# Gate, up and down projections as seven half-size products instead of eight

## The chip, the cores and the metric

The kernel runs on one core of one Trainium2 chip. Five engines matter: TensorE (PE in the profile, its weight loads apart as PEld), VectorE (DVE), ScalarE (ACT), GpSimd (POOL) and SyncE (SP), whose queue issues the DMA transfers here. The metric is the device time of one execution in microseconds, the median of several runs.

## What is computed

One decoder layer over 512 tokens with 2048 features, all in float32. The mixing sub-layer comes first; the change touches what follows it:

```python
x = x + g_m[:, None, :] * mix
h = modulate(rms_norm(x, norm_ffn_g[l]), sh_f, sc_f)
gate, up = jnp.split(h @ w_gu[l], 2, axis=-1)        # 2048 -> 2 x 5632
x = x + g_f[:, None, :] * ((jax.nn.silu(gate) * up) @ w_down[l])   # 5632 -> 2048
return rms_norm(x, final_norm_g)
```

`sh_f`, `sc_f` and `g_f` are columns of `silu(c) @ w_ada + b_ada` (the modulation columns).

## The kernel before

Features lie on the 128 partitions and the 512 tokens along the free dimension. A feature vector of 2048 is 16 tiles (`KT`), the hidden vector of 5632 is 44 (`FT`). Float32 products are made from float32r parts: `split_into` (L103 to L106) writes `hi` on ACT and the remainder `lo` on DVE, and `mm3` (L122 to L126) issues three matrix products, hi x hi, hi x lo and lo x hi, each of 128 x 128 weights by 512 columns. `load_split` (L112) loads up to 1024 columns of weights through SP's queue into one of the `raw` buffers and splits them, under `high_priority`, into `whi` and `wlo`; `gemm_steps` (L128) runs them over all k.

`channel` (L912) first ends the output projection (`project`), in which every second step also makes a quarter of one of the modulation columns 68 to 79; each finished tile of x1 is squared into `acc`. Then come the norm, `modulate` for 16 tiles of h, and four chunks of the hidden vector with 11 tiles each: for each tile 16 k of gate and 16 of up into two PSUM banks, `Silu`, the product with up and its split; then 16 output tiles of `down` over the chunk's 11 k, each added into x1 in SBUF with the gate column g_f (L969). In the first chunk the last 16 modulation columns are made beside gate and up. Last come the final norm, 16 multiplications (L975) and the stores (L977).

The program is traced in this order, and a list scheduler puts each engine's instructions in the order in which it expects them to be ready, earlier-traced and high-priority ones first. Each engine, and SP's queue, then runs its list strictly in that order and waits where data or a buffer isn't ready. A pool's tiles of one tag share its `bufs` buffers.

The memory pool `big` holds 32 tiles of 128 x 512, for h (hi and lo), later for the split y and for x1.

## Time and profile before

| | us |
|---|---|
| median of 3 runs | 2512.42 (2512.3 to 2514.79) |
| span of the profiled execution | 2515.8 |
| PE busy in it | 2413.9 |
| DVE busy | 1380.4 |
| ACT busy | 843.7 |
| POOL busy | 82.0 |

The span is that of one execution under the profiler, from the first to the last instruction; no other time of that execution is given. Busy time counts an engine's instructions with their overlaps once. PE's matrix products are pipelined: their starts are measured, their ends modelled, so the spacing of starts says how fast PE runs, not the recorded length of one.

### The profile page before, as it was taken

What the parts mean: (1) busy time and instruction counts of PE and PEld (TensorE: products, weight loads), DVE (VectorE), ACT (ScalarE), POOL (GpSimd) and SP (SyncE); (2) the same over time, 40 slices, a digit from 0 to 9 for tenths busy, and PEclk for the clock granted to TensorE, in tenths of its full rate; (3) what the DMA queues carried; (4) which work ended last, traced back from release to release, by engine and by line L of the source; (5) the groups of instructions that cost most, each with busy time, mean ns of one, the idle gap of its engine ahead of it and who ended that gap; (6) DMA issues with size and microseconds to landing.
All of it is one profiled execution on the core that took longest, in us unless ns stands there. A gap on an engine that the chain in (4) does not pass through costs nothing.

```text
span 2515.8 us, 30983 instructions
## 1 busy us (share of the span) xinstructions
PE 2413.9 (96%) x11560; PEld 1953.4 (78%) x11560; DVE 1380.4 (55%) x3111; ACT 843.7 (34%) x1340; POOL 82.0 (3%) x131
## 2 busy tenths in 40 slices
PE   5999999999999999899999999999999999999997
PEld 3677777877777886687788888888888888888885
DVE  7979898999969847854423322233322233222244
ACT  4357364455355333432222222222222222222221
POOL 0000111111101000000000000000000000000000
PEclk9999998999999999999999999999999999999998
DMA  8864444444342438366423332323333233333233
GB/s 304 308 219 130 148 128 143 131 152 144 125 135 81 143 108 283 119 195 194 160 90 95 108 100 93 101 83 98 106 98 99 89 92 105 101 93 100 85 95 112
DMA packets 138938, 333.22 MB, mean 132 GB/s; under 512 B 15458, under 2 KB 28898, under 8 KB 134690
## 3 DMA queue, kind: packets, MB, share of 16 engines
q1 hardware_dynamic: 138788, 331.25, 40.7%
q8 instruction: 90, 1.47, 0.2%
q14 instruction: 60, 0.49, 0.1%
HBM read 322.92 MB, written 7.87 MB: 131 GB/s over the span
## 4 chain that ended last, share of the span: by engine, by line
PE 72%; DVE 9%; DMA 7%; issue 1%; ACT 1%; SPq 0%; POOL 0%; DVEq 0%; ACTq 0%
PE ps_mm L124 10%; PE ps_mm L126 10%; PE ps_mm L125 10%; PE ps_gr L126 6%; PE ps_st L124 6%; PE ps_gr L124 6%; PE ps_st L126 6%; PE ps_gr L125 6%; PE ps_st L125 6%; DMA adaq<-in_w_ada 6%; DVE adaq L199 2%; DVE wlo L106 2%; DVE rw_xp L764 1%; DVE rw_x L766 1%; DMA wraw<-in_w_out 1%
## 5 line engine op out<-in xcount | busy, mean ns | idle before, releaser
L106 DVE TENSOR_TENSOR wlo<-wraw,whi 128x1024 fp32r<-128x1024 f32 (+2 forms) x552 | 496.7, 902 | 730.2 <-ACT whi L105 721.1
L105 ACT CAST whi<-wraw 128x1024 fp32r<-128x1024 f32 (+2 forms) x552 | 436.6, 792 | 1292.4 <-PE ps_mm L125 401.1
L124 PE MATMUL ps_mm<-hhi,whi 128*128 128x512 f32 x1020 | 417.1, 410 | 9.8 <-ACT hhi L251 7.2
L126 PE MATMUL ps_mm<-hhi,wlo 128*128 128x512 f32 x1020 | 407.2, 399 | 1.7 <-DVE wlo L106 1.6
L125 PE MATMUL ps_mm<-hlo,whi 128*128 128x512 f32 x1020 | 406.5, 399 | 0.8 <-DVE hlo L252 0.7
L124 PEld LDWEIGHTS ps_mm<-hhi,whi 128*128 128x128 f32 x1020 | 193.4, 190 | 53.2 <-ACT hhi L251 9.9
L125 PEld LDWEIGHTS ps_mm<-hlo,whi 128*128 128x128 f32 x1020 | 193.7, 190 | 43.4 <-DVE hlo L252 4.8
L126 PEld LDWEIGHTS ps_mm<-hhi,wlo 128*128 128x128 f32 x1020 | 193.8, 190 | 42.3 <-DVE wlo L106 3.0
L199 DVE SCALAR_TENSOR_TENSOR adaq<-adaq,cbq 128x512 f32<-128x512 f32 x256 | 173.5, 687 | 92.9 <-DMA adaq<-in_w_ada 85.1
L126 PE MATMUL ps_gr<-hhi,wlo 128*128 128x512 f32 x496 | 193.7, 390 | 3.1 <-DVE wlo L106 3.1
L126 PE MATMUL ps_st<-hhi,wlo 128*128 128x512 f32 x496 | 193.6, 390 | 2.0 <-DVE wlo L106 2.0
L124 PE MATMUL ps_st<-hhi,whi 128*128 128x512 f32 x496 | 194.0, 391 | 1.6 <-ACT hhi L251 1.6
L125 PE MATMUL ps_gr<-hlo,whi 128*128 128x512 f32 x496 | 193.5, 390 | 0.0
L125 PE MATMUL ps_st<-hlo,whi 128*128 128x512 f32 x496 | 193.5, 390 | 0.0
L124 PE MATMUL ps_gr<-hhi,whi 128*128 128x512 f32 x496 | 192.6, 391 | 0.0
L126 PEld LDWEIGHTS ps_gr<-hhi,wlo 128*128 128x128 f32 x496 | 93.4, 188 | 23.6 <-DVE wlo L106 4.1
L126 PEld LDWEIGHTS ps_st<-hhi,wlo 128*128 128x128 f32 x496 | 93.4, 188 | 21.8 <-DVE wlo L106 2.5
L124 PEld LDWEIGHTS ps_st<-hhi,whi 128*128 128x128 f32 x496 | 93.5, 188 | 21.6 <-ACT hhi L251 2.2
L125 PEld LDWEIGHTS ps_gr<-hlo,whi 128*128 128x128 f32 x496 | 93.7, 189 | 19.6
L124 PEld LDWEIGHTS ps_gr<-hhi,whi 128*128 128x128 f32 x496 | 93.7, 189 | 19.4
L125 PEld LDWEIGHTS ps_st<-hlo,whi 128*128 128x128 f32 x496 | 93.3, 188 | 19.8 <-DVE hlo L252 0.3
L766 DVE TENSOR_TENSOR rw_x<-rw_x,rw_xp 128x27 f32<-128x27 f32 (+23 forms) x496 | 94.7, 196 | 5.7
(312 smaller groups left out, 3809.6 us busy)
## 6 DMA issues: line engine op xcount, KB each, us to landing
wraw<-in_w_gu SPq DMA_DIRECT2D x176, 512.0 KB, 3.6
adaq<-in_w_ada SPq DMA_DIRECT2D x256, 256.0 KB, 3.3
wraw<-in_w_in SPq DMA_DIRECT2D x160, 256.0 KB, 3.0
ada<-in_w_ada SPq DMA_DIRECT2D x32, 1024.0 KB, 7.2
wraw<-in_w_down SPq DMA_DIRECT2D x64, 512.0 KB, 3.5
wraw<-in_w_out SPq DMA_DIRECT2D x64, 256.0 KB, 3.3
wraw<-in_w_down SPq DMA_DIRECT2D x64, 192.0 KB, 2.3
x<-in_x SPq DMA_DIRECT2D x32, 256.0 KB, 5.3
```

The costliest lines, as they stand in the source:

```text
L105: nc.scalar.copy(out=hi, in_=src)
L106: nc.vector.tensor_tensor(out=lo, in0=src, in1=hi.bitcast(F32), op=ALU.subtract)
L124: mm(ps, lhsT=w[0], rhs=x[0], start=start, stop=False)
L125: mm(ps, lhsT=w[0], rhs=x[1], start=False, stop=False)
L126: self.pe = mm(ps, lhsT=w[1], rhs=x[0], start=False, stop=stop).ins
L199: nc.vector.scalar_tensor_tensor(out=t, in0=t, scalar=1.0, in1=cb, op0=ALU.mult, op1=ALU.mult, accum_out=part[:, m, h:h + 1])
L764: tt(out=pr[:, :n, :j], in0=at[:, s + 1:, s:s + 1].to_broadcast([P, n, j]), in1=x[:, s:s + 1, :j].to_broadcast([P, n, j]), op=ALU.mult)
L766: tt(out=x[:, s + 1:, :j], in0=x[:, s + 1:, :j], in1=pr[:, :n, :j], op=ALU.add)
```

## The change

Gate, up and down are computed with a scheme of seven products (Strassen's, in Winograd's form) on 2 x 2 blocks: the tokens are cut into two halves of 256, the features (k) into two halves, and the columns into two, which are the gate and the up tile of one m, or the output tiles m and m + 8 of down. Eight block products become seven, of sums and differences of blocks.

- `group` makes one such pair of output tiles. It loads four blocks of weights (128 x 1024; in down 128 x 1024 or 128 x 896), forms four sums of them (two on POOL, two on DVE), splits seven blocks into hi and lo, multiplies each by 256 columns over n k (8 or 7), and combines the seven results on the way out of PSUM (one copy on ACT, seven additions and subtractions on DVE).
- `operands` splits the seven blocks on the activations' side, once for a stage: `from_h` for h, `from_s` for a chunk of the hidden vector. Their eight sums (tiles of 128 x 4 x 256) are made on POOL.
- h is modulated in halves of 256 tokens, in place in x1's tiles. x1 therefore goes to DRAM (`x1d`) and is loaded, updated and stored again by each down chunk; the hidden vector goes to DRAM too (`sd`) and is loaded by halves. There are three chunks of down (16, 14 and 14 tiles) where four were.
- The operands of a stage are made beside the last group of the stage before. The first two groups are interleaved product by product.
- The last 16 modulation columns are made beside groups 4 and after, two quarters in each.
- `big` holds 8 tiles of 128 x 4 x 512, which `quad_view` gives out by quarters. The weights' pool has 10 `raw` buffers of 1024 columns and three each of `whi` and `wlo`; it is opened before the end of the output projection.

```diff
+    def quad_view(self, k, name, dtype):
+        if k % 4 == 0:
+            self.quad[name] = self.big.tile([P, 4, S], dtype, tag="h", name=name)
+        return self.quad[name][:, k % 4]
...
-        self.big = ctx.enter_context(tc.tile_pool(name="big", bufs=32))
-        self.open_weights(ctx, "wm", 512, 3, 3)
-        self.wm = self.wp
+        self.big = ctx.enter_context(tc.tile_pool(name="big", bufs=8))
+        self.quad = {}
+        self.wmctx = ExitStack()
+        self.open_weights(self.wmctx, "wm", 512, 3, 3)
         self.psum = ctx.enter_context(tc.tile_pool(name="psum", bufs=1, space=PSUM))
...
+        self.wmctx.close()
+        self.open_weights(ctx, "wf", 1024, 10, 3)
+        self.fq = fq = ctx.enter_context(tc.tile_pool(name="fq", bufs=2))
+        self.acc = acc = fq.tile([P, S], F32, name="sqacc", bufs=1)
+        self.x1d = [self.dram.tile([P, S], F32, name=f"x1d{m}") for m in range(KT)]
...
+            def done(m):
+                self.square(acc, xt[m], m, fp)
+                nc.sync.dma_start(out=self.x1d[m], in_=xt[m])
+            self.after_project = done
+            mods = self.mod_steps(range(64 + 4, 80), fp, ("ft", 2, "ad", 4))
...
-        for cf in range(NC):
-            s = []
-            for f in range(FC):
-                m = cf * FC + f
-                pg, pu = ps(), ps()
-                self.gemm(pg, i["w_gu"][2 * m], h)
-                self.gemm(pu, i["w_gu"][2 * m + 1], h)
...
-            if cf == 0:
-                with self.tc.issue_after(last):
-                    self.mod_cols(range(80, 96), self.wm, ("raw", 3, "raw", 3))
-            for m in range(KT):
-                p = ps()
-                self.gemm(p, i["w_down"][cf, m], s)
-                stt(out=xt[m], in0=p, scalar=self.mod[:, 80 + m:81 + m], in1=xt[m],
-                    op0=ALU.mult, op1=ALU.add)
-                if cf == NC - 1:
-                    self.square(acc, xt[m], m, fp)
...
+        chunks = [(0, 8), (16, 7), (30, 7)]
...
+        def modulate(q, side):
+            sl = slice(side * 256, side * 256 + 256)
+            for z in range(4):
+                k = 4 * q + z
+                v = quads[q][:, z, sl]
+                stt(out=v, in0=v, scalar=self.cols[:, 16 + k:17 + k], in1=rstd[:, sl],
+                    op0=ALU.mult, op1=ALU.mult)
+                nc.scalar.activation(out=v, in_=v, func=AF.Identity, bias=self.mod[:, 48 + k:49 + k])
...
+        def from_h(p):
+            if p == 1:
+                modulate(0, 0)
+                modulate(1, 0)
+                return [view(0, 0), view(1, 0)]
+            if p == 2:
+                modulate(2, 0)
+                modulate(3, 0)
+                return [view(2, 0), view(3, 0)]
+            if p == 6:
+                for j in range(2):
+                    modulate(j, 1)
+                    modulate(2 + j, 1)
+                    t = self.staging()
+                    pool_tt(out=t, in0=view(j, 1), in1=view(2 + j, 1), op=ALU.subtract)
+                    pool_tt(out=view(j, 1), in0=view(j, 0), in1=view(j, 1), op=ALU.subtract)
+                    pool_tt(out=view(j, 0), in0=t, in1=view(j, 0), op=ALU.subtract)
+                    s1.append(t)
+                return [view(0, 0), view(1, 0)]
+            if p == 5:
+                return s1
+            if p == 7:
+                return [view(0, 1), view(1, 1)]
+            if p == 4:
+                return [view(2, 1), view(3, 1)]
+            s4 = [self.staging(), self.staging()]
+            for j in range(2):
+                pool_tt(out=s4[j], in0=view(2 + j, 0), in1=view(j, 0), op=ALU.add)
+            return s4
...
+                    if p in (1, 2, 4):
+                        r.append(load(p != 1, p == 4, j))
+                    elif p == 6:
+                        t, u = load(0, 1, j), load(1, 1, j)
+                        pool_tt(out=t, in0=t, in1=u, op=ALU.subtract)
+                        u = load(0, 0, j)
+                        pool_tt(out=u, in0=t, in1=u, op=ALU.subtract)
+                        kept.append(t)
+                        r.append(u)
+                        v = load(1, 0, j)
+                        pool_tt(out=v, in0=v, in1=u, op=ALU.add)
+                        nc.sync.dma_start(out=self.s4[j][:, :v.shape[1]], in_=v)
+                    elif p == 7:
+                        t, u = load(0, 0, j), load(0, 1, j)
+                        pool_tt(out=t, in0=t, in1=u, op=ALU.subtract)
+                        r.append(t)
+                    else:
+                        t = self.staging()[:, :min(4, n - 4 * j)]
+                        nc.sync.dma_start(out=t, in_=self.s4[j][:, :t.shape[1]])
+                        r.append(t)
...
+        def gu_end(m, g, u):
+            nc.scalar.activation(out=g, in_=g, func=AF.Silu)
+            nc.vector.tensor_tensor(out=g, in0=g, in1=u, op=ALU.mult)
+            nc.sync.dma_start(out=where[m], in_=g)
+        last = {}
+        def down_end(c):
+            def end(m, g, u):
+                for t, k in ((g, m), (u, m + 8)):
+                    x = fq.tile([P, S], F32, tag="x1", name="x1t", bufs=2)
+                    nc.sync.dma_start(out=x, in_=self.x1d[k])
+                    stt(out=x, in0=t, scalar=self.mod[:, 80 + k:81 + k], in1=x, op0=ALU.mult, op1=ALU.add)
+                    if c == len(chunks) - 1:
+                        self.square(acc, x, k, fq)
+                        last[k] = x
+                    if c < len(chunks) - 1 or m < 7:
+                        nc.sync.dma_start(out=self.x1d[k], in_=x)
+            return end
...
+        def gu_src(m):
+            a, b = i["w_gu"][2 * m], i["w_gu"][2 * m + 1]
+            return a[:, :1024], b[:, :1024], a[:, 1024:], b[:, 1024:]
...
+        mods = self.mod_steps(range(80, 96), fq, ("ft", 2, "x1", 2))
+        self.ngroup = 0
+        order = (1, 2, 6, 5, 7, 4, 3)
+        g0, g1 = self.group(stages[0], 0), self.group(stages[0], 1)
+        for p in order[:-1]:
+            self.operands(stages[0], p)
+            next(g0)
+            next(g1)
+        self.operands(stages[0], 3)
+        for g in (g0, g1):
+            for _ in g:
+                pass
+        for z, st in enumerate(stages):
+            nxt = stages[z + 1] if z + 1 < len(stages) else None
+            for m in range(2 if z == 0 else 0, st["count"]):
+                g = self.group(st, m)
+                final = m == st["count"] - 1
+                for p in order:
+                    if p == 3 and final and nxt is None:
+                        self.reload(last)
+                    next(g, 0)
+                    if final and nxt is not None:
+                        self.operands(nxt, p)
+                    if z == 0 and m >= 4 and p in (6, 4):
+                        next(mods, 0)
...
+        for k in (7, 15, *[k for k in range(KT) if k not in (7, 15)]):
+            stt(out=last[k], in0=last[k], scalar=self.vec("final_norm_g", k), in1=rstd,
+                op0=ALU.mult, op1=ALU.mult)
+            nc.sync.dma_start(out=self.out[:, k], in_=last[k])
...
+    def reload(self, last):
...
+            v = self.quad_view(k, "xend", F32)
+            if k not in (7, 15):
+                self.nc.sync.dma_start(out=v, in_=self.x1d[k])
+                last[k] = v
...
+    def staging(self):
+        t = self.wp.tile([P, self.wc], F32, tag="raw", name="stage", bufs=self.wb[0])
+        return t.rearrange("p (k n) -> p k n", n=256)
...
+    def operands(self, stage, p):
+        at = {1: 0, 2: 2, 6: 4, 5: 6, 7: 8, 4: 10, 3: 12}[p]
+        out = []
+        for j, src in enumerate(stage["get"](p)):
+            if 4 <= at + j < 10:
+                t = self.cp.tile([P, 4, S], F32R, tag="c", name="comb")
+            else:
+                t = self.big.tile([P, 4, S], F32R, tag="h", name="comb")
+            n = src.shape[1]
+            t = t.rearrange("p k n -> p (k n)").rearrange("p (h k n) -> p h k n", h=2, n=256)
+            self.split_into(t[:, 0, :n], t[:, 1, :n], src)
+            out.append(t)
+        stage["ops"][p] = out
...
+    def group(self, stage, m):
+        nc, tc = self.nc, self.tc
+        tt, pool_tt = nc.vector.tensor_tensor, nc.gpsimd.tensor_tensor
+        n = stage["n"]
+        N = n * P
+        par = self.ngroup % 2
+        self.ngroup += 1
+        raw = []
+        for src in stage["src"](m):
+            t = self.wp.tile([P, self.wc], F32, tag="raw", name="wraw", bufs=self.wb[0])[:, :N]
+            raw.append(t)
+        for z in (0, 2, 1, 3):
+            nc.sync.dma_start(out=raw[z], in_=stage["src"](m)[z])
+        b11, b12, b21, b22 = raw
+        def product(tag, p, w):
+            with tc.high_priority():
+                hi = self.wp.tile([P, self.wc], F32R, tag="whi", name="whi", bufs=self.wb[1])
+                lo = self.wp.tile([P, self.wc], F32R, tag="wlo", name="wlo", bufs=self.wb[1])
+                self.split_into(hi[:, :N], lo[:, :N], w)
+            ops = stage["ops"][p]
+            ps = self.ps(tag)[:, :256]
+            for k in range(n):
+                sl = slice(k * P, k * P + P)
+                o = ops[k // 4]
+                self.mm3(ps, (hi[:, sl], lo[:, sl]), (o[:, 0, k % 4], o[:, 1, k % 4]), k == 0, k == n - 1)
+            return ps
+        def tmp(tag):
+            return self.ev.tile([P, 256], F32, tag=tag, name="ev_" + tag, bufs=1)
+        g = self.ev.tile([P, S], F32, tag="g", name="ev_g")
+        u = self.ev.tile([P, S], F32, tag="u", name="ev_u")
+        ps = product("mm", 1, b11)
+        a = tmp("a")
+        nc.scalar.copy(out=a, in_=ps)
+        yield
+        ps = product("gr", 2, b21)
+        tt(out=g[:, :256], in0=ps, in1=a, op=ALU.add)
+        yield
+        with tc.high_priority():
+            pool_tt(out=b11, in0=b11, in1=b12, op=ALU.add)
+            t2 = self.wp.tile([P, self.wc], F32, tag="t2", name="t2", bufs=1)[:, :N]
+            tt(out=t2, in0=b11, in1=b22, op=ALU.add)
+        ps = product("ch", 6, t2)
+        with tc.high_priority():
+            tt(out=b21, in0=t2, in1=b21, op=ALU.add)
+        b = tmp("b")
+        tt(out=b, in0=ps, in1=a, op=ALU.add)
+        yield
+        p5 = product(("st", "y")[par], 5, b11)
+        tt(out=u[:, :256], in0=p5, in1=b, op=ALU.subtract)
+        yield
+        with tc.high_priority():
+            pool_tt(out=b12, in0=b12, in1=b22, op=ALU.add)
+        ps = product("mm", 7, b12)
+        c = tmp("c")
+        tt(out=c, in0=ps, in1=b, op=ALU.add)
+        tt(out=u[:, 256:], in0=p5, in1=c, op=ALU.subtract)
+        yield
+        ps = product("gr", 4, b21)
+        tt(out=g[:, 256:], in0=ps, in1=c, op=ALU.add)
+        yield
+        ps = product("ch", 3, b22)
+        tt(out=u[:, :256], in0=ps, in1=u[:, :256], op=ALU.add)
+        stage["end"](m, g, u)
...
-    wd = a["w_down"][0]
-    o["w_down"] = np.stack([_tiles(wd[c * 1408:(c + 1) * 1408]) for c in range(4)])
+    o["w_down"] = _tiles(a["w_down"][0])
```

More of the change, by code (lines that the diff above doesn't have):

```diff
@@ L400, in filler @@
             self.ya = [self.load_y(k, self.big) for k in range(8)]
-            self.x1 = [self.big.tile([P, S], F32, tag="h", name="x1") for k in range(KT)]
+            self.x1, self.x1q = [], []
+            for k in range(KT):
+                self.x1.append(self.quad_view(k, "x1", F32))
+                if k % 4 == 0:
+                    self.x1q.append(self.quad["x1"])
             for k in range(KT):
@@ new lines, in from_s, with load, get @@
+        def from_s(c):
+            n = chunks[c][1]
+            kept = []
+            def load(e, side, j):
+                t = self.staging()[:, :min(4, n - 4 * j)]
+                nc.sync.dma_start(out=t, in_=self.sd[c, e, j][:, :, side * 256:side * 256 + 256])
+                return t
+            def get(p):
+                if p == 5:
+                    return kept
+                r = []
+                for j in range(2):
+                    if p in (1, 2, 4):
[15 more added lines that the diff above has]
+                    else:
+                        t = self.staging()[:, :min(4, n - 4 * j)]
+                        nc.sync.dma_start(out=t, in_=self.s4[j][:, :t.shape[1]])
+                        r.append(t)
+                return r
+            return get
@@ new lines, in channel @@
+        self.s4 = [self.dram.tile([P, 4, 256], F32, name=f"s4{j}") for j in range(2)]
+        def gu_end(m, g, u):
[15 more added lines that the diff above has]
+            return end
@@ new lines, in channel @@
+        for c in range(len(chunks)):
+            stages.append(dict(n=chunks[c][1], count=8, src=down_src(c), get=from_s(c), end=down_end(c), ops={}))
+        mods = self.mod_steps(range(80, 96), fq, ("ft", 2, "x1", 2))
[7 more added lines that the diff above has]
+        self.operands(stages[0], 3)
```

90 lines of the change are left out of this document (45 added, 45 removed).

## The prediction

> **What bounds the kernel now.** I read the page's busy times first, then the busy times by stretch from the last product of the mixing part to the end.
>
> ```profile
> span 2515.8 us, 30983 instructions
> PE 2413.9 (96%) x11560; PEld 1953.4 (78%) x11560; DVE 1380.4 (55%) x3111; ACT 843.7 (34%) x1340; POOL 82.0 (3%) x131
> ...
> 1000.00:1038.50 38.50, 37.68 (x162) 29.66 (x160) 31.26 (x78) 13.78 (x22) 0.00 (x0) 1.00 0.66 221
> 1038.50:1046.00 7.50, 2.69 (x17) 2.23 (x16) 3.90 (x9) 2.91 (x5) 0.00 (x0) 0.83 0.00 0
> 1046.00:1080.00 34.00, 32.91 (x133) 26.10 (x134) 29.78 (x47) 17.62 (x23) 0.00 (x0) 0.94 0.25 78
> 1080.00:1260.00 180.00, 173.31 (x759) 141.67 (x758) 86.69 (x168) 41.64 (x48) 0.00 (x0) 1.00 0.58 186
> 1260.00:2494.50 1234.50, 1234.50 (x5447) 1021.96 (x5445) 382.75 (x412) 288.08 (x350) 0.00 (x0) 1.00 0.31 95
> 2494.50:2515.80 21.30, 3.49 (x17) 3.03 (x16) 13.12 (x23) 2.18 (x3) 0.00 (x0) 0.57 0.53 197
> ```
>
> (Stretch, then busy us and count of PE, weight loads, DVE, ACT, POOL, then clock, DMA share, GB/s.) The part that the change rewrites runs from 1038.5 to 2494.5 us: **1456 us**. For 1234 of them PE never stops; DVE is busy 31% of it, ACT 23%, POOL never. One load-and-multiply pair of 512 columns takes 1234.5 / 5447 = 226.6 ns. The code issues (44 x 2 x 16 + 4 x 16 x 11) x 3 = 6336 pairs, 1436 us; the other 20 are the norm (7.5) and the start of gate and up. So PE's number of pairs times its pace is the bound, and fewer columns can pay if the shorter pair is really shorter and the other engines keep up.
>
> **PE after the change.** A group (gate and up tile of one m, or two output tiles) issues 7 products x 8 k x 3 = 168 pairs of 256 columns; the 16 groups with n=7 issue 147. 52 x 168 + 16 x 147 = 11088 pairs. No row shows this form with 256 columns, so I bound it, from below by float32 products with as large a load.
>
> ```profile
> 610.98 0.30 PEld L710 LDWEIGHTS ps_y<-rw_rkt,bd_v 128*128 128x128 f32 x2
> 611.09 0.33 PE L710 MATMUL ps_y<-rw_rkt,bd_v 128*128 128x64 f32 x2
> ...
> 630.66 0.97 PEld L643 LDWEIGHTS ps_gr<-rw_ar,bd_k 128*128 128x128 f32 x8
> 630.77 1.06 PE L643 MATMUL ps_gr<-rw_ar,bd_k 128*128 128x128 f32 x8
> ...
> 1047.06 0.63 PE L125 MATMUL ps_st<-hlo,whi 128*128 128x512 f32 x1
> ...
> 1047.48 0.63 PE L126 MATMUL ps_st<-hhi,wlo 128*128 128x512 f32 x1
> ...
> 1047.91 0.63 PE L124 MATMUL ps_st<-hhi,whi 128*128 128x512 f32 x1
> ```
>
> A load is recorded with about 190 ns, but two of L710 fit into 300 and eight of L643 into 970: a new one every 110 ns, whatever the columns multiplied (64 or 128). That is the floor: 112 ns by L643. Above it: just after the norm, where the clock column falls to 0.83 and 0.94, pairs start 425 ns apart, PE at half clock. That is 212 ns of streaming at full clock; the other 14 of 226.6 appear at full clock only, which looks like a limit on the rate of columns, not a fixed part. Then 256 columns take **113.3 ns**, and PE needs 11088 x 0.1133 = 1256 us (19.0 a group, 16.7 with n=7). If there is a fixed part, the two clocks give 226.6 = s + c and 425 = 2s + c, c = 28, so 127 ns at most. I take 113.3, next to the L643 row. The Trainium skill, "TensorE: Matmul & The Clock Gate", section "Back-to-back issue gap", has N/2.4 + 2.5 ns, 109 for 256 columns; by it the PE sum would be 1210 us, an estimate; its 216 for 512 is not met here (226.6).
>
> **DVE, ACT and POOL after it.** Every product now splits its own 128x1024 weights: 7 x 1.05 us on ACT, with a 256-column copy and a Silu that are each shorter than one split (under 9 of 19 us, so ACT isn't the bound), and on DVE:
>
> ```profile
> L106 DVE TENSOR_TENSOR wlo<-wraw,whi 128x1024 fp32r<-128x1024 f32 x240 | 293.8, 1225 | 451.8 <-ACT whi L105 445.8
> L106 DVE TENSOR_TENSOR wlo<-wraw,whi 128x512 fp32r<-128x512 f32 x232 | 158.9, 686 | 51.8 <-ACT whi L105 48.8 <-PE ps_mm L126 0.9 <-issue 0.4
> ...
> L105 ACT CAST whi<-wraw 128x1024 fp32r<-128x1024 f32 x240 | 252.8, 1054 | 786.8 <-PE ps_gr L125 196.7 <-PE ps_st L125 196.1 <-PE ps_mm L125 191.8
> ...
> L649 DVE TENSOR_TENSOR rw_rkt<-ps_gr,cons 128x256 f32<-128x256 f32 x16 | 6.8, 425 | 0.3
> ...
> L975 DVE SCALAR_TENSOR_TENSOR x<-x,vecs,ps_ch 128x512 f32<-128x512 f32 x16 | 10.6, 741 | 1.6 <-PE ps_ch L240 1.6
> ...
> 2501.37 10.62 DVE L975 SCALAR_TENSOR_TENSOR x<-x,vecs,ps_ch 128x512 f32<-128x512 f32 x16 [1.58 <-PE ps_ch L240]
> ...
> L199 DVE SCALAR_TENSOR_TENSOR adaq<-adaq,cbq 128x512 f32<-128x512 f32 x256 | 173.5, 687 | 92.9 <-DMA adaq<-in_w_ada 85.1
> ```
>
> The sixteen of L975 span 10.62 us, one every 0.66 though each takes 0.74: DVE overlaps neighbours by 0.08, which I take off each. A gate/up group: 7 splits and 2 sums of weights, 9 x 1.145 = 10.3; seven reads of PSUM of 256 columns, 7 x 0.345 = 2.4; one 512-column multiply 0.6: **13.3 us**. Modulation columns (64 x 0.69, two a group) add 1.1 on average. Down groups have two x1 updates (as L975, 0.66 each) instead of the multiply: 14.1. With n=7 a split has 896 columns, 1.09 us between the two L106 rows, less 0.08: 12.9.
>
> POOL adds 128x1024 weights twice a group. The trace has only small one-input operations of it:
>
> ```profile
> L775 POOL TENSOR_SCALAR bd_xt<-rw_xs x64: 517/527/1017, 275.1 to 885.0; 32x128 f32<-32x128 f32 x64
> ...
> L616 POOL TENSOR_SCALAR bd_a<-rw_ar x32: 844/990/1830, 213.4 to 849.4; 64x256 f32<-64x256 f32 x32
> ...
> 213.39 2.97 POOL L616 TENSOR_SCALAR bd_a<-rw_ar 64x256 f32<-64x256 f32 x2 [23.34 <-DVE rw_ar L609]
> 213.83 0.69 DVE L590 TENSOR_TENSOR rw_a<-rw_a,rw_kk 128x512 f32<-128x512 f32 x1
> 214.43 0.89 DVE L584 SCALAR_TENSOR_TENSOR rw_t<-mix_r,vecs,mix_k 128x512 f32<-128x512 f32 x1
> ...
> 603.21 3.00 POOL L775 TENSOR_SCALAR bd_xt<-rw_xs 32x128 f32<-32x128 f32 x4 [18.98 <-DVE rw_xs L771]
> ...
> 604.46 0.77 DVE L106 TENSOR_TENSOR wlo<-wraw,whi 128x512 fp32r<-128x512 f32 x1
> ```
>
> From 0.52 (128 elements) to 0.84 (256) is 2.55 ns each: 2.8 us for 1024, and about twice that if the second input costs as much again. Beside DVE they get in each other's way: the same POOL form takes up to 1.83 us, and a DVE operation that should take 0.69 took 0.89. That is 0.2 us for 256 elements read, so 2 x 1024 read would cost DVE 1.6 us an add; bounds 0 and the whole 2.8. With 1.6, DVE's 13.3 + 1.1 + 3.2 = 17.6 stays under PE's 19.0; n=7: 12.9 + 2.8 = 15.7 under 16.7. So PE still sets the pace, narrowly.
>
> **What waits.** The hi and lo buffers are three deep, so the split for a product may start two products (5.4 us) before it, and takes 1.05 + 1.15. For product 6 it is preceded by a chain: product 1's split must have read b11, POOL adds b12 (2.8), DVE adds b22 (1.15), then ACT and DVE split. Measured from the release of product 1's buffer: 2.2 + 2.8 + 1.15 + 2.2 = 8.4 us against four products, 10.9. The 2.5 of slack goes when POOL and DVE hold each other up or an eviction sits ahead on DVE's queue. Behind the waiting sum on DVE stand the eviction of the product just finished and the lo splits of 6, then 5; behind the add of b11 on POOL stands that of b12, for product 7. So product 6 is late first, then 5. I charge 0.7 us a group, 48 us in 68 groups; bounds 0 and 2 us (136).
>
> Between stages the operands of the next one are made: 14 splits (15 us of DVE) and 8 adds on POOL, in two groups' time where DVE has about 3 us free: 15 + 8 x 0.5 (shut out, mostly under waits) - 3 = **16 us**, three times 48; bounds 7 and 35 each. At the start, 32 half modulations (11), 14 splits (16), 8 adds, and the first two groups' 27 fall on DVE: 54, with 12 adds x 0.8 = 10 of hindrance 64, against 38 of PE; 2 us of weight splits can be done before the norm: 24 us late (10 to 48), in place of 12 before. The norm stays, 7.5.
>
> Loads:
>
> ```profile
> GB/s 304 308 219 130 148 128 143 131 152 144 125 135 81 143 108 283 119 195 194 160 90 95 108 100 93 101 83 98 106 98 99 89 92 105 101 93 100 85 95 112
> ...
> wraw<-in_w_gu SPq DMA_DIRECT2D x176, 512.0 KB, 3.6
> ```
>
> Four of these a group are 2 MB in 19 us, 110 GB/s where the highest slice has 308. Each group's result is stored from SP's queue, so the store waits there for the group's end with later loads behind it; ten buffers hold two and a half groups, which covers the 3.6 us many times: nothing. Before the norm, x1 also goes to DRAM: 4.2 MB into a stretch that moves 221 GB/s, and the modulation columns have 4 buffers for 11: +8 us (0 to 15). The tail after the last product has two updates, two squares instead of one: +2. The larger tiles in the mixing part free later: nothing by my count, its loads lie under products.
>
> **Sum.** 1256 + 48 + 48 + 24 + 7.5 = 1384 for 1456: -72; +8 +2: -62. The profiled span of 2515.8 lies 3.4 over the median of 2512.4, so 2515.8 - 62 - 3.4 = **2450 us**; own range 2390 to 2500. 0.2% (5 us) is about what can be told from no change.
>
> **Rivals.** *A fixed part in the pair* (120 to 127 ns). PE 1331 to 1413; slack grows, so the lateness falls to 14 and 7, the stages to 40 and 36, the start to 22 and 20: 1414 to 1484, that is 2480 to 2549. For it: 14 ns unexplained. Against: they vanish at half clock.
>
> *POOL shuts DVE out for the whole add* (the one that ends slower). DVE then needs 13.3 + 1.1 + 5.6 = 20.0 a group, over PE's 19.0: DVE sets the pace. 44 x 20.0 + 8 x 19.7 + 16 x 17.8 = 1322, + 48, stages 3 x 35 = 105, start 54 + 12 x 2.8 - 2 - 38 = 48, norm 7.5: 1530, + 10: **2597**. Between 1.6 (2450) and 2.8 (2597) the gain is gone at about 2.1 us an add. For it: the 1.83 us; against: beside four of the 0.52 us POOL operations a 512-column split went from 0.69 to 0.77 only, where a lock for their whole length could have added 0.5. The Trainium skill speaks for it: "SBUF — State Buffer", section "Who interferes with whom", says that a DVE instruction with two SBUF inputs and a GpSimd one that reads SBUF lock each other out for the whole instruction. Here the small operations show less than that; no row has a long one. "GPSIMD Engine Reference", section 3.1, has 4497 ns for 2048 columns, so 2.25 for 1024, an estimate, which under that lock would give about no change.
>
> *All hides*: no lateness, stages 7 each, start 15: 1300, so 2366. *The change doesn't shorten the pair*: it keeps its recorded 190 ns load, 11088 x 0.19 = 2107, about 3190; L643's 112 speaks against.
>
> **Chances.** Forecast 0.42, fixed part 0.18, shut-out 0.27, all hides 0.10, no shorter pair 0.03. The forecast gives 0.40 faster and 0.02 same; the fixed part 0.08, 0.03 and 0.07; the shut-out 0.26 slower and 0.01 same; the rest by sign: faster 0.58, same 0.06, slower 0.36. The range 2370 to 2600 leaves out the pair that is no shorter, half of "all hides" and 0.12 of the shut-out.
>
> **What would show it.** In the profile after: 168 pairs a group at 113 ns in unbroken stretches (120 and over is the first rival; 190 the last); POOL's add at 2.3 to 2.8, and wlo splits still at 1.23 us with idle time before them (a mean well above, and DVE near 100%, is the second); PE waits on wlo before product 6; idle PE of some 16 us at the three changes of stage. I am wrong if these holes are several times that, or if DVE has no idle time in the groups.

## The result, and the profile after

The changed kernel takes **2676.07 us** (median; 2670.67 to 2679.86), the kernel before, on the same chip, 2512.36: a ratio of 1.0654, 95% interval 1.0635 to 1.0674. The forecast was 2450 with a range of 2370 to 2600: wrong in sign, and outside the range. First the page's busy times, then the busy times by stretch (columns as in the prediction).

```profile
span 2672.3 us, 42602 instructions
PE 2369.8 (89%) x16312; PEld 2140.5 (80%) x16312; DVE 2133.0 (80%) x3874; ACT 1092.5 (41%) x1591; POOL 561.6 (21%) x299
```

```profile
0.00:1078.70 1078.70, 970.96 (x5192) 762.38 (x5192) 868.16 (x2436) 487.26 (x896) 87.36 (x133) 0.97 0.52 166
1078.70:1094.00 15.30, 4.08 (x18) 3.59 (x17) 13.61 (x24) 6.30 (x11) 4.97 (x2) 0.64 0.42 141
1094.00:1164.40 70.40, 47.81 (x336) 46.49 (x337) 57.50 (x75) 40.13 (x58) 24.83 (x10) 0.79 0.29 91
1164.40:2647.30 1482.90, 1342.99 (x10754) 1324.46 (x10752) 1178.87 (x1316) 555.98 (x624) 444.44 (x155) 0.96 0.45 146
2647.30:2672.30 25.00, 3.96 (x17) 3.56 (x16) 14.90 (x26) 2.81 (x4) 0.00 (x0) 0.55 0.48 179
```

Every part grew, not only the rewritten one. By the starts of matrix products:

| stretch | before | after | more |
|---|---|---|---|
| to the last product of the projection | 1038.2 | 1078.4 | 40.2 |
| from there to the first product of the channel part | 7.8 | 15.6 | 7.8 |
| first to last product of the channel part | 1448.2 | 1553.1 | 104.9 |
| from there to the end | 21.6 | 25.3 | 3.7 |

The sum is 156.6, the two spans differ by 156.5. The third row is the one that should have shrunk. Timeline of PE in a quiet group (start, recorded length):

```profile
1499.89 0.28 PE L126 MATMUL ps_mm<-comb,wlo 128*128 128x256 f32 x1
1500.01 0.28 PE L124 MATMUL ps_mm<-comb,whi 128*128 128x256 f32 x1
1500.13 0.28 PE L125 MATMUL ps_mm<-comb,whi 128*128 128x256 f32 x1
1500.25 0.28 PE L126 MATMUL ps_mm<-comb,wlo 128*128 128x256 f32 x1
```

Pairs start **120 ns** apart, not 113.3; 11088 of them are 1330.6 us, and the rest of the 1553.1, 222.5 us, is lateness. From the starts of the groups' first products it divides into: the first two groups, 70.4 where PE needs 40.3 (30); groups 3 to 10, which take 24.2 to 27.8 where 20.16 is PE's time (48); the quiet groups, which have nothing else beside them, 20.90 each, and 18.55 for 17.64 with n=7 (41 in 52 groups); the last group of a stage with the first of the next, three times 34.5, 33.3 and 35.4 more than PE needs (103). Three views show what these are made of. First POOL and DVE around a quiet group's weight sums:

```profile
1496.00 2.41 POOL L1199 TENSOR_TENSOR wraw<-wraw 128x1024 f32<-128x1024 f32 x1 [14.97 <-DVE wlo L106]
1498.49 3.44 POOL L1212 TENSOR_TENSOR wraw<-wraw 128x1024 f32<-128x1024 f32 x1
...
1496.62 0.42 DVE L1219 TENSOR_TENSOR ev_g<-ps_gr,ev_c 128x256 f32<-128x256 f32 x1 [0.70 <-PE ps_gr L126]
1498.44 1.22 DVE L1201 TENSOR_TENSOR t<-wraw 128x1024 f32<-128x1024 f32 x1 [1.40 <-POOL wraw L1199]
1499.59 3.42 DVE L106 TENSOR_TENSOR wlo<-wraw,whi 128x1024 fp32r<-128x1024 f32 x1
1503.04 1.22 DVE L1204 TENSOR_TENSOR wraw<-t,wraw 128x1024 f32<-128x1024 f32 x1
```

An add on POOL takes 2.41 us alone and 3.44 where it meets DVE, and the split that begins beside it takes 3.42, not 1.22: it ends at 1503.01, 1.08 after POOL does. The eviction at 1496.62, which reads one operand from PSUM, runs during POOL's first add in its usual 0.42. The long split is product 2's, and of PE's waits (total, times, longest) this one comes in nearly every group; `ps_gr` also holds product 4, but 63 of the 65 are product 2's:

```profile
PE ps_gr L126 <- DVE wlo L106: 60.4, 65, 4.3
```

Second, the modulation steps (duration min/median/max, first and last start):

```profile
L199 DVE SCALAR_TENSOR_TENSOR adaq<-adaq,cbq x62: 672/691/2854, 1116.5 to 1366.3; 128x512 f32<-128x512 f32 x62
...
  DMA adaq<-in_w_ada: 31.0, 27
```

The code writes them two to a group from m=4 on, but DVE's order has 62 of the 64 between 1116 and 1366 us and the other two before, and DVE stands idle 31 us in front of them for their loads. These are the slow groups, eight in 209.2 us; of the quiet ones after them 31 take 648.3, by the busy times:

```profile
1185.50:1394.70 209.20, 179.53 (x1346) 177.30 (x1345) 164.52 (x245) 65.64 (x73) 49.04 (x18) 0.90 0.51 160
1394.70:2043.00 648.30, 633.07 (x5213) 626.76 (x5213) 504.49 (x529) 252.41 (x279) 181.78 (x63) 1.00 0.35 114
```

Third, a change of stage, in the timelines of SP's queue and of PE (`stage` is staging: a `raw` buffer lent to a tile of activations):

```profile
2105.16 0.33 SPq L1060 DMA_DIRECT2D s<-ev_g  x1
2105.89 0.82 SPq L1049 DMA_DIRECT2D stage<-s  x2
2106.76 1.39 SPq L1170 DMA_DIRECT2D wraw<-in_w_down  x3
...
2093.91 0.28 PE L126 MATMUL ps_ch<-comb,wlo 128*128 128x256 f32 x1
2113.64 0.58 PE L124 MATMUL ps_mm<-comb,whi 128*128 128x256 f32 x1 [19.44 <-ACT whi L105]
2114.02 0.42 PE L125 MATMUL ps_mm<-comb,whi 128*128 128x256 f32 x1
```

PE stands still for 19.4 us: the new stage's first weights are loaded only at 2106.8, behind the last staging tile and the last group's store in SP's queue.

### The profile page after: what moved, and what is told of

It reads as the page before. It is cut to its first block, busy times and chain, and to the rows that moved or that the text cites. A ratio compares the mean times of both kernels' runs of the same rounds, so it can differ in the third digit from the quotient of the medians.

```text
span 2672.3 us, 42602 instructions
## 1 busy us (share of the span) xinstructions
PE 2369.8 (89%) x16312; PEld 2140.5 (80%) x16312; DVE 2133.0 (80%) x3874; ACT 1092.5 (41%) x1591; POOL 561.6 (21%) x299
## 4 chain that ended last, share of the span: by engine, by line
issue 37%; PE 16%; DVE 14%; POOL 14%; DMA 12%; ACT 1%; SPq 1%; POOLq 0%; DVEq 0%; ACTq 0%
POOL wraw L1212 7%; DMA adaq<-in_w_ada 6%; POOL wraw L1199 6%; DVE wlo L106 3%; PE ps_mm L124 3%; PE ps_mm L125 3%; PE ps_mm L126 3%; DVE adaq L199 2%; DMA wraw<-in_w_down 1%; DMA stage<-s 1%; DVE rw_xp L776 1%; DVE rw_x L778 1%; DVE comb L106 1%; DMA cbq<-csilu 1%; POOL stage L1041 1%
## 5 line engine op out<-in xcount | busy, mean ns | idle before, releaser
L106 DVE TENSOR_TENSOR wlo<-wraw,whi 128x1024 fp32r<-128x1024 f32 (+2 forms) x639 | 783.5, 1227 | 107.4 <-ACT whi L105 101.4
L1199 POOL TENSOR_TENSOR wraw<-wraw 128x1024 f32<-128x1024 f32 (+1 forms) x68 | 163.0, 2397 | 1158.2 <-DVE wlo L106 963.1
L126 PE MATMUL ps_gr<-comb,wlo 128*128 128x256 f32 x1056 | 314.3, 298 | 60.1 <-DVE wlo L106 60.1
L124 PE MATMUL ps_mm<-comb,whi 128*128 128x256 f32 x1056 | 303.3, 287 | 66.2 <-ACT whi L105 62.6
L124 PE MATMUL ps_ch<-comb,whi 128*128 128x256 f32 x1056 | 303.3, 288 | 21.5 <-ACT comb L105 21.5
L126 PE MATMUL ps_ch<-comb,wlo 128*128 128x256 f32 x1056 | 305.6, 289 | 14.4 <-DVE wlo L106 14.4
L124 PE MATMUL ps_gr<-comb,whi 128*128 128x256 f32 x1056 | 306.4, 290 | 0.0
L125 PE MATMUL ps_gr<-comb,whi 128*128 128x256 f32 x1056 | 306.4, 290 | 0.0
L126 PE MATMUL ps_mm<-comb,wlo 128*128 128x256 f32 x1056 | 303.2, 287 | 2.7 <-DVE wlo L106 2.7
L125 PE MATMUL ps_ch<-comb,whi 128*128 128x256 f32 x1056 | 303.2, 287 | 0.5 <-DVE comb L106 0.5
L125 PE MATMUL ps_mm<-comb,whi 128*128 128x256 f32 x1056 | 302.7, 287 | 0.5 <-DVE comb L106 0.5
L126 PEld LDWEIGHTS ps_gr<-comb,wlo 128*128 128x128 f32 x1056 | 210.7, 200 | 73.3 <-DVE wlo L106 73.3
L1212 POOL TENSOR_TENSOR wraw<-wraw 128x1024 f32<-128x1024 f32 (+1 forms) x68 | 224.1, 3296 | 5.7 <-DMA adaq<-in_w_ada 0.7
L126 PEld LDWEIGHTS ps_ch<-comb,wlo 128*128 128x128 f32 x1056 | 206.7, 196 | 17.3 <-DVE wlo L106 15.8
L125 PEld LDWEIGHTS ps_gr<-comb,whi 128*128 128x128 f32 x1056 | 210.4, 199 | 0.0
```

The source lines that it names most:

```text
L106: nc.vector.tensor_tensor(out=lo, in0=src, in1=hi.bitcast(F32), op=ALU.subtract)
L124: mm(ps, lhsT=w[0], rhs=x[0], start=start, stop=False)
L125: mm(ps, lhsT=w[0], rhs=x[1], start=False, stop=False)
L126: self.pe = mm(ps, lhsT=w[1], rhs=x[0], start=False, stop=stop).ins
L1199: pool_tt(out=b11, in0=b11, in1=b12, op=ALU.add)
L1212: pool_tt(out=b12, in0=b12, in1=b22, op=ALU.add)
```

## The experiments

Where nothing else is said, an experiment is one run; runs of one kernel scatter by up to 15 us (2516.2 to 2530.7 is the widest of the repeated ones), so the table has the channel part by itself too, which the scatter of the part before it doesn't enter. The runs stand on several chips; the kernel before took 2508 to 2512 us on each.

| kernel | time us | first to last product of the channel part |
|---|---|---|
| after | 2676.1 | 1553.1 |
| e3_group_adds_dve | 2591.3 | 1466.1 |
| e12_idle_pool_adds | 2635.9 | 1512.4 |
| e4_stage_adds_dve | 2631.5 | 1515.1 |
| e10_no_pool | 2536.3 | 1418.6 |
| e5_early_loads | 2648.6 | 1528.5 |
| e6_mods_in_step | 2665.8 | 1549.8 |
| e9_mods_behind_dve | 2625.9 | 1507.3 |
| e7_ad11 | 2663.3 | 1551.8 |
| e14_small_pieces | 2674.0 | 1554.1 |
| c1_together | 2514.5 | 1403.8 |
| c2_loads_ahead_of_seven | 2521.6 | 1415.3 |
| e13_no_stage_sums | 2504.6 | 1389.7 |
| c3_sums_early | 2492.9 | 1381.8 |
| c4_sums_and_loads_early | 2493.7 | 1381.8 |

### The pair of 256 columns

In the kernel before, `mm3` of the channel part issues each product in parts of its columns:

```diff
+        for a, b in self.cut:      # ((0, 256), (256, 512)) or ((0, 128), (128, 512))
+            sl = slice(a, b)
+            mm(ps[:, sl], lhsT=w[0], rhs=x[0][:, sl], start=start and a == 0, stop=False)
+            mm(ps[:, sl], lhsT=w[0], rhs=x[1][:, sl], start=False, stop=False)
+            self.pe = mm(ps[:, sl], lhsT=w[1], rhs=x[0][:, sl], start=False, stop=stop and b == S).ins
```

> The kernel before, with each of its 6,336 pairs of 512 columns in the channel sub-layer issued as two of 256. Fixed part (226.6 ns = s + c, 120 = s/2 + c, so c = 13.4): 12,672 x 0.120 = 1,520.6 where 6,336 x 0.2266 = 1,435.7 stood, so +85 us, about 2,597, and a pace of 0.120 in the records. Rate alone (the forecast's 113.3): no change, 2,512. That the 0.120 is something of the changed kernel (its operands' layout, POOL beside it): no change here either.

> As the one before, but 128 and 384 columns. Fixed part of 13.4 ns: 53.3 + 13.4 = 66.7 and 159.9 + 13.4 = 173.3, together 240.0, so +85 us again, 2,597. A floor under a pair's pace (the weight load, 0.19 to 0.20 in the records, would let no pair begin sooner than 120 after the one before): 120 + 170 = 290, +402 us, 2,914. Rate alone: 2,512.

The halves took 2610.56 us beside 2508.11 for the kernel before: +102, where the fixed part had +85 and the forecast's rate none. The 128 and 384 columns took 2948.6: +440, near the floor's +402 and far from +85. In their traces the channel part, first to last product, takes 1531.1 and 1874.5 us where 1448.2 stood: +83 and +426; the rest of the +102 lies ahead of it (its first product comes 10 us later) or in the scatter of whole runs. PE's timeline of the halves, then of the uneven parts:

```profile
1499.74 0.28 PE L127 MATMUL ps_st<-hlo,whi 128*128 128x256 f32 x1
1499.86 0.28 PE L128 MATMUL ps_st<-hhi,wlo 128*128 128x256 f32 x1
1499.98 0.28 PE L126 MATMUL ps_st<-hhi,whi 128*128 128x256 f32 x1
```

```profile
1499.80 0.22 PE L126 MATMUL ps_gr<-shi,whi 128*128 128x128 f32 x1
1499.86 0.27 PE L127 MATMUL ps_gr<-slo,whi 128*128 128x128 f32 x1
1499.97 0.27 PE L128 MATMUL ps_gr<-shi,wlo 128*128 128x128 f32 x1
1500.08 0.40 PE L126 MATMUL ps_gr<-shi,whi 128*128 128x384 f32 x1
1500.31 0.34 PE L127 MATMUL ps_gr<-slo,whi 128*128 128x384 f32 x1
1500.49 0.34 PE L128 MATMUL ps_gr<-shi,wlo 128*128 128x384 f32 x1
1500.66 0.22 PE L126 MATMUL ps_gr<-shi,whi 128*128 128x128 f32 x1
```

The 0.12 belongs to the pair, whichever kernel issues it. Both theories hold, each in its place. Pairs of 384 start 175 ns apart: with 226.6 and 120.0 for 512 and 256, a column costs (226.6 - 120.0) / 256 = 0.416 ns and a pair 13.4 more; that gives 173.3 for 384. Pairs of 128 start 111 to 112 apart, not 66.7: a floor, which the forecast had from L643. As 128 columns go below 120, the floor doesn't make the 120. (One start in six is early, 60 ns, and one late, 230; only the sum of six, 0.86, is safe.) The Trainium skill, "TensorE: Matmul & The Clock Gate", section "Wait — 56ns, not 53.3ns?", has columns / 1.2 exactly while the clock is low, and columns / 2.4 plus 2.5 ns once it is up. The form agrees, a fixed part that is there at full clock alone; the size doesn't, 13.4 ns here for 2.5.

### POOL's additions

```diff
-        tt, pool_tt = nc.vector.tensor_tensor, nc.gpsimd.tensor_tensor
+        tt = pool_tt = nc.vector.tensor_tensor
```

> The changed kernel with the two additions on POOL in each group of weights done on DVE. POOL shutting DVE out for its whole add: DVE's splits are 1.2 us everywhere, the wait for product 2's split goes, a steady group falls from 20.9 to 20.2, 68 x 0.75 = 51 us less, about 2,625, and some of the start goes too. Rival, DVE has no room or its order sets the wait: DVE carries 2 x 1.2 us more a group, a group stays at 20.9 or grows, 2,676 or more.

2591.3, 85 less: the quiet groups took exactly PE's 20.16 and 17.64 (41 us of it). Groups 3 to 10, with the modulation steps still drawn forward, fell to 21 to 22 (32 more, counting the four groups after them, which hold the last of these steps), so much of their slowness was POOL too. The changes of stage took 13 less. DVE had the room. Busy times of a quiet stretch in e3, where PE never stops; 554.0 / 4619 = 119.9 ns:

```profile
1446.00:2000.00 554.00, 554.00 (x4619) 554.00 (x4618) 449.01 (x523) 226.73 (x248) 0.00 (x0) 1.00 0.39 118
```

Was it the shut-out, or only a shorter chain from sum to split? The adds were put back with nobody waiting for them, behind products 5 and 7:

```diff
+        nc.gpsimd.tensor_tensor(out=b11, in0=b11, in1=b11, op=ALU.add)
...
+        nc.gpsimd.tensor_tensor(out=b12, in0=b12, in1=b12, op=ALU.add)
```

> e3_group_adds_dve (2,591) with two POOL additions a group put back that nobody waits for: they double, in place, the raw weights of products 5 and 7 once these are split (the values are read by nothing after). If an add on POOL shuts DVE out for its whole time: DVE's splits of 3.4 us come back beside them, and a group goes from 20.16 back to between 20.5 and 21, 2,610 to 2,650. If e3's gain was only the shorter chain from the sum to its split: groups stay at 20.16, 2,591.

2635.9, 45 more than without them, within the band, but not where it was expected: the quiet groups stayed at 20.16, since these adds fall where DVE has time to spare, and the 45 came in the groups with modulation steps (+32), at the changes of stage (+5), in the last five groups (+6) and at the start (+3). The shut-out itself is plain, with no data between the two engines. Timelines of DVE and of POOL:

```profile
1506.41 1.88 DVE L106 TENSOR_TENSOR wlo<-wraw,whi 128x1024 fp32r<-128x1024 f32 x1 [0.48 <-ACT whi L105]
...
1509.29 2.12 DVE L106 TENSOR_TENSOR wlo<-wraw,whi 128x1024 fp32r<-128x1024 f32 x1 [0.54 <-ACT whi L105]
...
1504.93 2.28 POOL L1209 TENSOR_TENSOR wraw<-wraw 128x1024 f32<-128x1024 f32 x1 [13.41 <-DVE wlo L106]
1508.43 1.89 POOL L1215 TENSOR_TENSOR wraw<-wraw 128x1024 f32<-128x1024 f32 x1 [1.23 <-DVE wlo L106]
```

POOL ends at 1507.21 and 1510.32, the two splits at 1508.29 and 1511.41, each 1.08 to 1.09 later: a split that comes during the add runs after it, for 1.08 of its 1.22 us. So it is throughout: in the traces of after and e12, all 151 splits and sums of 128x1024 that begin during an add on POOL and outlast it end 1.08 to 1.09 us after it. Evictions are not held: 61 of product 4's begin during an add of after and take 0.41 to 0.43 us, as they do without one. The Trainium skill, "SBUF — State Buffer", section "Who interferes with whom", says that a DVE instruction with two SBUF inputs and a GpSimd one that reads SBUF shut each other out for a whole instruction, and the longest split agrees: 3437 ns with POOL's adds of weights and operands, 1228 in c1_together, which has none. The splits' rows (min/median/max) after, and in c1_together:

```profile
L106 DVE TENSOR_TENSOR wlo<-wraw,whi x639: 549/1214/3437, 29.1 to 2640.8; 128x1024 fp32r<-128x1024 f32 x82, 128x512 fp32r<-128x512 f32 x54, 128x896 fp32r<-128x896 f32 x24
```

```profile
L106 DVE TENSOR_TENSOR wlo<-wraw,whi x639: 550/1215/1228, 28.7 to 2487.3; 128x1024 fp32r<-128x1024 f32 x82, 128x512 fp32r<-128x512 f32 x54, 128x896 fp32r<-128x896 f32 x24
```

For the 0.74 us of a quiet group of the changed kernel, e3 and e12 don't tell the shut-out from the chain. The first rows of POOL and DVE above have both in a row before product 2's split: DVE stands idle 1.40 us for POOL's first add, and its split then loses 2.20 us to the second. PE waits 0.49 us for that split, so by this count taking away either would have been enough; e3 took away both.

### The last modulation columns

```diff
-                        next(mods, 0)
+                        with tc.issue_after(self.pe):      # e6; self.dve, the eviction of product 6 or 4, in e9
+                            next(mods, 0)
```

> The changed kernel with each of the 64 steps of the last modulation columns held in DVE's order behind the matmul at which the code writes it, two to a group in groups 4 to 35. If DVE's waits for these loads, drawn together into groups 2 to 10, make those eight groups 24 to 28 us: they fall to 21, some 42 us less, 2,634. If weight loads, POOL or the clock make those groups long: no change, 2,676.

> The changed kernel with the 64 modulation steps held behind DVE's own evictions of products 6 and 4, at which the code writes them (e6_mods_in_step held them behind a matmul and DVE's order stayed as it was). If their being drawn together into groups 2 to 10 makes those groups 24 to 28 us: those fall to 21, 42 us less, and two steps of 0.75 in each of 32 groups cost nothing (2,634) or 0.75 a group in the wait for product 2's split (2,658). If they cost the same wherever they stand: 2,676.

e6 says nothing on the question: the order behind a matmul didn't move DVE's steps, which stayed at 1110 to 1359 us. e9 moved them, and took 2625.9, the channel part 46 us shorter; groups 3 to 10 fell to 20.91, and none of those that now hold two steps grew. So these groups had two causes that overlap, the loads (46 us back in e9) and POOL (32 in e3), of 48 in all. The steps now run from 1211 to 1874 us, with no idle time before them:

```profile
L199 DVE SCALAR_TENSOR_TENSOR adaq<-adaq,cbq x64: 676/680/685, 1211.3 to 1874.3; 128x512 f32<-128x512 f32 x64
```

### The changes of stage

```diff
-        pool_tt = nc.gpsimd.tensor_tensor
+        pool_tt = nc.vector.tensor_tensor        # e4: in channel, the operands' sums
...
+                    if final and nxt is not None and p == 4:      # e5; p == 7 in c2
+                        ahead = self.group(nxt, 0)
+                        next(ahead)                                # the loads alone
```

> The changed kernel with the sums of the operands (start and three changes of stage) on DVE; the groups' own additions stay on POOL. If POOL's chain of 2.4 to 5.6 us adds holds the stage buffers and so the next stage's weight loads: the three gaps of 20 to 24 us before a stage's first product fall to about 10, the first two groups from 70 to about 50, together some 50 us less, 2,626. If the buffers and SP's order alone set it, or DVE is what is late: under 15 us less, 2,661 or more.

> The changed kernel with the loads of a stage's first group of weights issued ahead of the staging loads for products 4 and 3, no longer behind them. If the gaps of 19.7, 19.9 and 24.0 us before a stage's first product are these loads standing behind staging on SP and in the ring of ten buffers: about 9 us less each, 27 in all, 2,649. If the first product waits for its activations: no change, 2,676.

> The changed kernel with all of POOL's additions of the channel sub-layer on DVE (e3_group_adds_dve and e4_stage_adds_dve together). If the two are separate costs: 85 and 45 us less, 2,546. If DVE is then what is late at start and stage changes: the gaps go back to 20, about 2,580. If each gain was the same lock seen twice: about 2,590.

e4 took 2631.5, 45 less (38 in the channel part): the gaps before the stages' first products fell from 19.7, 19.9 and 24.0 only to 15.8, 14.7 and 17.2, but the whole changes gave 31 us and the start 8. e5 took 2648.6, 27 less as expected (25 in the channel part): the gaps fell to 12.5, 12.7 and 16.9. e10, with e3's and e4's edits, took 2536.3, 140 less than after, where the two had 85 and 45: separate costs, and no gain counted twice. So the gap had two causes in a row, POOL's chain of adds and, behind it, the weight loads in SP's queue. That the chain acts by holding the staging buffers, as expected of e4, was not shown by itself.

All edits together (with e7's, below), and then the loads a step earlier still, product 3's activations being staged behind product 7 of the new group:

> The changed kernel with all additions on DVE, the first weights of a stage loaded ahead of the staging for products 4 and 3, eleven buffers for the modulation beside the projection, and the 64 last modulation steps behind DVE's evictions. By the single runs 85 + 45 + 27 + 13 and some 10 us less, of which 15 of the 27 may be in the 45 already: 2,496 to 2,511, the kernel before within half a per cent. If the gains overlap more: 2,540.

> As c1_together, but a stage's first weights are loaded ahead of the staging for product 7, and product 3's activations are staged behind product 7 of the new stage's first group, so that ten buffers are enough. If the 10.8, 9.4 and 9.7 us that are left before a stage's first product are still these loads: they fall to 2 or 3, 22 us less, 2,492, 0.7% under the kernel before. If what is left is the split and the clock at the restart: 2,514. If product 3 then waits for its activations, 3 to 6 us a stage come back: 2,505.

c1 took 2514.49 us where the kernel before took 2510.16, ratio 1.0011 (1.0000 to 1.0023): level, and 3 us above the band expected. c2 took 2521.56, ratio 1.0053 (1.0035 to 1.0071). Its gaps did fall, to 1.3, 2.6 and 2.7 us, and yet the stretches grew: the last group of gate and up and the next two took 80.2 us, 74.5 in c1, 60.5 being PE's. The idle time had moved, not gone. In c1 the first two of these groups had kept DVE busy for 53.8 of 54.1 us:

```profile
1977.40:2031.50 54.10, 42.94 (x336) 42.23 (x336) 53.79 (x56) 29.05 (x31) 0.00 (x0) 0.87 0.84 286
```

To see what bounds the stretch, the sums were left out (e13, which splits the tiles as they are loaded):

```diff
-                        pool_tt(out=t, in0=t, in1=u, op=ALU.subtract)
...
-                        pool_tt(out=v, in0=v, in1=u, op=ALU.add)
```

> c2_loads_ahead_of_seven (2,521) without the eight sums and differences on DVE at each of the three changes of stage (the sums of s are left out, the tiles are split as loaded). If DVE's work is what makes the last group and the first two of a stage 80 us where 60.5 would be PE alone: 8 x 1.25 = 10 us less a change, 30 in all, 2,491. If the loads (270 to 290 GB/s there) or PE's half clock after each wait set it: under 3 us a change, 2,512 or more.

Busy times of the three groups, first in c2, then without the sums:

```profile
1969.50:1990.80 21.30, 19.53 (x161) 19.12 (x160) 20.32 (x21) 12.24 (x14) 0.00 (x0) 1.00 0.81 272
1990.80:2023.00 32.20, 24.31 (x156) 22.80 (x154) 28.64 (x30) 14.80 (x16) 0.00 (x0) 0.84 0.86 287
2023.00:2049.70 26.70, 24.66 (x193) 24.59 (x193) 24.02 (x32) 8.68 (x9) 0.00 (x0) 0.94 0.51 166
```

```profile
1979.50:2000.90 21.40, 19.00 (x157) 18.59 (x156) 19.67 (x23) 13.84 (x15) 0.00 (x0) 1.00 0.76 256
2000.90:2026.10 25.20, 22.77 (x171) 22.16 (x172) 23.30 (x26) 13.70 (x15) 0.00 (x0) 0.93 1.03 382
2026.10:2048.50 22.40, 22.05 (x182) 21.63 (x181) 21.21 (x27) 8.58 (x9) 0.00 (x0) 1.00 0.54 172
```

DVE is busy 20.3, 28.6 and 24.0 us of the three, 73 in all, and without the sums 64; the stretch goes from 80.2 to 69.0, the three changes together 28 us shorter, the 30 expected of DVE. (The time fell by only 17; the part ahead of the channel part came out 9 us longer in this run.) The loads are not the bound: they ran faster, 382 GB/s for 287. So the sums were moved into quiet groups, where DVE has 3 us to spare (449 of 554 us busy in e3's stretch above), and put by in DRAM:

```diff
+                with tc.issue_after(self.dve):
+                    tt(out=y, in0=x, in1=y, op=ALU.subtract)
+                    tt(out=x, in0=w, in1=x, op=ALU.subtract)
+                    tt(out=w, in0=y, in1=w, op=ALU.subtract)
+                    tt(out=v, in0=v, in1=w, op=ALU.add)
+                for p, t in ((5, y), (7, x), (6, w), (3, v)):
+                    ...
+                    nc.sync.dma_start(out=d, in_=t)
```

> As c1_together, with the sums of the next stages' activations computed ahead, in groups 18, 20, 32 and 34 of gate and up and groups 2 and 4 of the first down stage, and put by in DRAM; a change of stage only loads and splits. If DVE is what bounds the changes and has 3 us of room in each quiet group: 8 x 1.25 = 10 us less at each of three changes, some 25 to 30 in all, 2,487. If DVE's work costs the same wherever it stands: 2,514. If the gap before a stage's first product is then left with the weight loads alone: 2,500.

> As c3_sums_early, with a stage's first weights loaded ahead of the staging for product 7, as in c2_loads_ahead_of_seven. Where DVE no longer bounds the stretch, the earlier loads should count, 5 us a change: 2,475. If the loads and the staging share the same 270 to 380 GB/s and only change places: as c3_sums_early.

c3 took **2492.89 us** beside 2509.64 for the kernel before, ratio 0.9929 (0.9911 to 0.9946): 0.7% below the kernel before, with an interval that leaves out 1, 6.8% below the changed one, and 22 us below c1, where 25 to 30 were expected. c4, with the loads earlier, took 2493.66, ratio 0.9940 (0.9923 to 0.9957): the loads no longer matter. What is left of lateness in c3 is 31 us at the three changes and 20 at the start, 1381.8 - 1330.6. Around the first change DVE is still busy 22.8 of 23.0 us and then 21.8 of 22.0 (1973 to 1996 and 1996 to 2018), now with the splits.

### The part before

```diff
-            mods = self.mod_steps(range(64 + 4, 80), fp, ("ft", 2, "ad", 4))
+            mods = self.mod_steps(range(64 + 4, 80), fp, ("ft", 2, "ad", 11))     # e7
...
-        kp = self.wc // P
+        kp = 4                                                                   # e14, beside e7's edit
...
-        self.big = ctx.enter_context(tc.tile_pool(name="big", bufs=32))
+        self.big = ctx.enter_context(tc.tile_pool(name="big", bufs=8))           # e8, in the kernel before, with quad_view
```

> The changed kernel with eleven buffers, as before, where the change left four for the modulation columns loaded beside the output projection. If DVE's waits for these loads make the projection 123 us where 108 stood: it falls to about 110, 2,663. If the reuse of released memory by the new pools sets it: no change, 2,676.

> e7_ad11 (2,663) with the output projection's weights loaded and split in pieces of 512 columns, as before, where the change makes them 1,024. If the larger pieces are the rest of the projection's lateness (the idle 6.7 us before its second half): 6 to 9 us less, 2,655. If the reused memory sets it: 2,663.

> The kernel before with only the activations, y and the residual held in eight tiles of four columns, where 32 tiles of one were. If a tile of four, freed only when its last quarter is read, delays the mixing part: its last product comes up to 26 us later than 929.8, 2,528 to 2,538. If the rest of the change (memory taken early for the channel sub-layer, residual written out) makes the later head: 2,512.

By the traces the 40 us are two pieces: the last product of the mixing part comes at 955.4 where 929.8 stood (26), and the projection ends 123.0 us after it where 108.4 stood (15). Eight kernels with the same code up to there (after, e3, e4, e5, e6, e9, e10, e12) have the first anywhere from 947.7 to 959.0.

e7 took 2663.3, the 13 us expected, but by luck: the second piece fell to 119.6, not to about 110, and 7 us came in the mixing part, within its scatter. The second piece takes 122.5 to 125.8 us in the eight kernels and 118.6 to 123.9 in the seven with eleven buffers (e7, e13, e14, c1 to c4): some 3 us. e14 took 2674.0, not 2655; its second piece took 120.4, so smaller pieces don't explain the rest. e8 took 2526.5 beside 2509.9, with the mixing part ending at 942.7, where the old tiles have 929.8, 932.3 and 936.4 (before, e2, e1), and a second piece of 109.0: the tiles of four cost 6 to 13 us of the first piece, an estimate from one run each; that e8 took 7 us more than any run of the kernel before (2519.4) speaks for it. Some 25 to 31 us of the 40 stay open; the early opening of the channel part's buffers and the stores of x1 were not tried by themselves.

## Why the prediction was wrong, step by step

- **"A limit on the rate of columns, not a fixed part. Then 256 columns take 113.3 ns"**: this step failed. The 14 ns do vanish at half clock, with 256 columns too: in e5, just before a gap and with 0.50 in the clock column, pairs start 0.213 us apart, twice 0.107 with nothing on top. But that didn't exclude a fixed part at full clock: e1 and the changed kernel both show 120.0. PE's term was 1331, not 1256: +75, the largest miss, and the lower edge of the first rival.

```profile
2087.67 0.41 PE L126 MATMUL ps_ch<-comb,wlo 128*128 128x256 f32 x1
2087.88 0.41 PE L124 MATMUL ps_ch<-comb,whi 128*128 128x256 f32 x1
2088.09 0.41 PE L125 MATMUL ps_ch<-comb,whi 128*128 128x256 f32 x1
```

- **"2 x 1024 read would cost DVE 1.6 us an add"**: failed as well. DVE waits out what is left of the add, up to the whole 2.4 us; small one-input operations were no guide. The row that gave the 0.2 us was misread, too: that operation (L584) takes 0.74 to 0.75 us by itself, not 0.69, so it had lost 0.14. The second rival was right on the mechanism, and on the changes of stage (35 each; 34.5, 33.3 and 35.4 came), but not on the groups: DVE doesn't set their pace (504.5 us busy of 648.3), because one add of the two meets DVE at work and the other finds it idle or at an eviction, which it doesn't hold.
- **The rivals were priced one at a time, and both came.** They act on different engines, so neither excluded the other. The 2597 of the second was reckoned against a PE that needs 19.0 us a group.
- **0.7 us of lateness a group**: right in size (0.74 to 0.91, 41 us where 48 stood), on the wrong product: 2, behind POOL's two adds, not 6. The mechanism was off here and the sum came out by luck.
- **Changes of stage, 16 us each**: 34 (+55). POOL's chain of adds was one cause (e4, 31 us), and once it was gone DVE's own work (e13, c3); another was **"ten buffers ... covers the 3.6 us many times: nothing"**: true in the groups, false at a change, where the same ten buffers hold staging tiles and SP's queue has staging ahead of the weights (e5, 27 us).
- **Modulation columns, 1.1 us a group on average**: the average held, the place didn't. DVE's order drew them into eight groups, in front of their loads, where they and POOL's adds cost 48 us (e9: 46 back). Nothing in the forecast asked where each step stands in DVE's queue.
- **The start**, 24: 30. **Norm to first product**, no more than before: 7.8 more. **Before the norm**, +8: 40; "nothing by my count" for the larger tiles was 6 to 13 (e8), the four buffers some 3 (e7), and the rest isn't explained. **The tail**, +2: 3.7.

Against the forecast, the terms add 75 + 48 + 55 + 6 + 8 + 32 + 2 - 7 = 219 us of the 226 missed; the other 7 are the place of the profiled span beside the median, 3.4 over it before and 3.8 under it after. What it had right: the chip can do these products in less time than before, if the other engines keep up (1331 for 1436), and DVE's room was narrow.

## What to carry to other kernels

Price a smaller matrix product by a measured pace at that size: of the 180 us that seven products for eight should save of 1436, the fixed 13 ns a pair took 74 before any other engine was asked. Before a sum is given to GpSimd, ask whether VectorE works with two inputs from SBUF at that time: here VectorE, though busy for 80% of the span and GpSimd for 21%, did the same sums at no cost in the quiet groups, and with less lateness at the changes of stage. And where idle time only moves when its last cause is removed (c2), look for the engine whose busy time fills the stretch (VectorE, 53.8 of 54.1 us in c1), and move its work to where it has room (c3).

## What the runs showed of the hardware beside this

- A pair's 13.4 ns are there at full clock with 256 and 512 columns, and with 384 to within 2 ns; at half clock they are not, with 256 columns (0.213 us in e5) and 512 (0.425 in the kernel before).
- A wait costs PE more than its length: in the quiet groups of the changed kernel, where PE is recorded idle for 0.49 us before product 2's split, a group is 0.74 us longer (the idle time is counted from a modelled end), and after the 19.4 us of the first change of stage the first two pairs start 0.38 apart, where 0.21 is the pace at half clock and 0.12 at full.
- The row of 382 GB/s in e13, over 25 us, is the most that any stretch shown here moved; the forecast's 308 is the highest of 40 slices of 63 us.
